# Seven block products for eight in the second output projection of a two-layer decoder step

## The chip, the cores and the metric

The kernel runs on one core of a Trainium2 chip. The metric is the device time of one execution in microseconds (us). The kernel before took 2897.57 us as the median of three runs (2897.03 to 2903.0).

## The reference, cut to what matters

One inference step of a two-layer decoder, for a prompt of 2048 positions and for 8 samples of 4 positions each, all in f32, with a model width of 1024 and a branch width of 2048. Layer 0 is gated linear attention. Layer 1 is sliding-window attention with 32 query heads in 4 groups. Each layer ends in an output projection from 2048 to 1024; the second one is the place of the change:

```python
BRANCH_WIDTH = EXPAND * D_MODEL          # 2 * 1024
...
def swa_out(o, gate, w_out):
    bsz, seq_len = o.shape[:2]
    return (o.reshape(bsz, seq_len, BRANCH_WIDTH) * jax.nn.silu(gate)) @ w_out
...
hp = hp + swa_out(swa_banded(q_p, k_p, v_p, b_sinks[j]), g_p, b_w_out[j])
...
hs = hs + swa_out(attend(q_s, k_s, v_s, pos_s, kpos_s, b_sinks[j]), g_s, b_w_out[j])
```

So for the prompt a [2048 x 2048] matrix (attention output times gate) is multiplied with `b_w_out` [2048 x 1024], the residual stream is added, and the result is the output `y`; the 32 sample rows go the same way into `ys`.

## The kernel before, in words

Every f32 operand of a large matmul is held as two f16 parts, hi and lo, and each product is three f16 matmuls (hi hi, hi lo, lo hi: `PASSES`, line 280). `split` (187) makes the parts: ScalarE (ACT) copies to hi, VectorE (DVE) or GpSimd (POOL) subtracts to lo. The prompt is cut into 16 chunks of 128 rows.

*Order of the work.* A scheduler orders the instructions of each engine by a simulated timeline; `behind` (171) lowers the priority of steps that can wait. In the attention of layer 1 the order of the matmuls is pinned to that of the program (`pin`, 1479).

1. *Layer 0* (line 895 on): 16 blocks (4 heads, 4 blocks of 512 rows each).
2. *First output projection* (1076 to 1089 and 1470): for each chunk 2 halves of 512 columns, 48 matmuls of 128x512 each. Its results are stored to `hd` and normed for layer 1.
3. *Layer 1, attention* (1501 to 1534): for 4 groups of 8 heads, 16 chunks each, so 64 blocks. While block t is attended, the query and gate projections of block t+3 are woven in as filler (`ORDER`, 1480). At the end of a block `last` (1276) makes `og`, the gated output [128 x 512] of this group; `spill_og` (617) splits it and stores hi and lo to `ogd2[c]` in DRAM (tile name oge). The last three turns of the loop have no projection left; their filler is the second output projection of chunks 0 to 2, first half.
4. *Second output projection* (1005, and 1538 to 1552): `out_steps` loads a chunk with 4 transposing DMAs (line 1012, 2 for hi and 2 for lo) and runs 16 k-tiles x 3 passes = 48 matmuls of 128x512 into one PSUM tile; `b_finish` (1481) adds the residual from `hd` and stores 512 columns of `y`. First half 0 for all 16 chunks, then half 1 for all, so 32 such units in all. The samples go through `out_sample` (1051): 4 tiles x 16 k-tiles x 2 small matmuls for each half.

*Weights ahead of time.* The weights of layer 1 are split long before they are used. `Unit.prepare` (237) gives two steps for each unit: load 256 KB of raw f32 (tile wraw, 3 buffers), split into a tile pst (2 buffers), and store that from POOL's queue (line 245) to a DRAM tile `pre`. They are taken in order from one list `prep` (835, 856): 8 steps for rope tables, 72 for the query, key, value and gate weights, 32 for `b_w_out`. `some(PR[j])` (936) takes 1, 4 or 2 of them per chunk in blocks of layer 0, 63 in all; the remaining 49 are taken 5 per chunk by chunks 4 to 13 of the first output projection (1086). `Unit.fetch` (249) loads a unit later, 512 KB at a time, into a tile W (12 buffers). Chunks 0 to 3 of the first output projection (1079 to 1083) are woven with the end of layer 0's last block and its samples, without such steps.

## Time and profile before

| | |
|---|---|
| median of 3 runs | 2897.57 us |
| the profiled execution, own time | 2899.76 us |
| its span, first to last instruction | 2898.0 us, mean granted clock of TensorE 0.989 |
| TensorE matmuls (PE) busy | 2769.2 us, 96% of the span |
| DVE, ACT, POOL busy | 1661.5, 1386.7, 1012.0 us |
| bytes moved by DMA | 393.86 MB, mean 136 GB/s |

The profile is one execution. PE is the matmul engine and PEld its weight loads, which run beside the matmuls; SP issues most DMAs. Times are counted from the first instruction. Layer 0 lasts to about 1180 us, the first output projection to about 1520 us, the attention to about 2590 us, and the second output projection alone takes the rest. A row of a view names the line of the kernel, the engine, the operation and the tiles (out<-in); "DMA share" in a table of stretches is the mean busy share of the 16 DMA engines, and can pass 1 where several transfers overlap on one.

### The profile page before, as it was taken

How to read it: one execution, taken by the hardware profiler on the slowest of the kernel's cores; microseconds unless marked ns; L12 is line 12 of the kernel's file. 1: busy time of each engine (PE TensorE's matmuls, PEld its weight loads, DVE VectorE, ACT ScalarE, POOL GpSimd, SP SyncE). 2: the span in 40 equal slices, each digit the busy share in tenths (PEclk: the TensorE clock that was granted, in tenths of full speed). 3: DMA queues.
4: the chain of work that ended last, by engine and by line, in shares of the span. 5: the costliest groups of instructions: out<-in, count | busy, mean ns of one | idle time of the engine just before them, and what ended most of it. 6: DMA issues, size and time to landing. Idle time of an engine off the chain costs nothing.

```text
span 2898.0 us, 51309 instructions
## 1 busy us (share of the span) xinstructions
PE 2769.2 (96%) x19198; PEld 1401.8 (48%) x19198; DVE 1661.5 (57%) x3543; ACT 1386.7 (48%) x3289; POOL 1012.0 (35%) x1407
## 2 busy tenths in 40 slices
PE   6899999999999999997999999999899999999999
PEld 4445444444454444444444555555555555544444
DVE  5766787687768775333214666677777767730000
ACT  6655655465556554333213555566666666620000
POOL 1241233222322221022105676566566557510000
PEclk9999999999999999998999999999999999999999
DMA  8351344124313524799866565767866777898874
GB/s 211 85 124 44 88 120 128 37 84 151 97 41 101 162 69 114 158 238 260 186 167 142 109 131 122 192 119 129 170 114 130 169 132 138 162 214 170 182 148 96
DMA packets 813331, 393.86 MB, mean 136 GB/s; under 512 B 687760, under 2 KB 740952, under 8 KB 813048
## 3 DMA queue, kind: packets, MB, share of 16 engines
q1 hardware_dynamic: 802040, 361.14, 56.3%
q0 software_dynamic: 8960, 29.37, 2.8%
q8 instruction: 150, 2.46, 0.4%
q14 instruction: 101, 0.83, 0.1%
q10 hardware_dynamic: 2080, 0.07, 0.0%
HBM read 132.61 MB, written 101.25 MB: 81 GB/s over the span
## 4 chain that ended last, share of the span: by engine, by line
PE 59%; DVE 10%; ACT 9%; DMA 9%; issue 7%; POOL 5%; SPq 1%; POOLq 0%; ACTq 0%; DVEq 0%
PE pj L99 45%; PE tr L99 6%; PE o L99 4%; PE kv L99 3%; DMA pre<-pst 2%; ACT o L1237 2%; DMA wraw<-in_a_w_in_dram 2%; DVE v L195 1%; DMA pst<-v 1%; ACT v L194 1%; PE lev L99 1%; DVE o L1232 1%; POOL pre L245 1%; DVE W L195 1%; DVE lev L1232 1%
## 5 line engine op out<-in xcount | busy, mean ns | idle before, releaser
L99 PE MATMUL pj<-W,uT 128*128 128x512 f16 x6600 | 1529.0, 381 | 6.6 <-DVE sg L475 3.4
L99 PEld LDWEIGHTS <-uT 128*128 128x128 f16 x8224 | 788.1, 98 | 892.6 <-issue 49.3
L99 PE MATMUL tr<-W,uT 128*128 128x512 f16 x1536 | 365.5, 379 | 0.0
L183 POOL TENSOR_SCALAR rs_m<-ss 128x1 f32<-128x1 f32 (+3 forms) x190 | 44.6, 235 | 757.7 <-ACT og L608 243.6
L1237 ACT ACTIVATE o<-o,mx 128x256 f32<-128x256 f32 (+1 forms) x384 | 168.6, 439 | 181.5 <-DVE mx L1232 172.1
L192 POOL TENSOR_TENSOR ogT<-og,ogT 128x512 f16<-128x512 f32 x132 | 162.1, 1228 | 168.3 <-ACT ogT L191 163.8
L99 PEld LDWEIGHTS <-X 128*128 128x128 f16 x2496 | 159.9, 98 | 120.9 <-issue 20.7
L99 PE MATMUL pj<-uT,W 128*128 128x512 f16 (+1 forms) x912 | 187.0, 356 | 27.1 <-DMA uT<-ogT 23.6
L1232 DVE CUSTOM_DVE_ANT_0 o<-o,madd,nsink 128x256 f32<-128x256 f32 (+1 forms) x384 | 184.0, 479 | 46.8 <-PE o L99 41.8
L195 DVE SCALAR_TENSOR_TENSOR v<-o,v 128x512 f16<-128x512 f32 (+1 forms) x192 | 129.0, 672 | 116.3 <-ACT v L194 98.4
L184 POOL TENSOR_TENSOR rs_r<-rs_m,mhalf 128x1 f32<-128x1 f32 (+2 forms) x186 | 185.5, 998 | 14.7
L99 PEld LDWEIGHTS <-W 128*128 128x128 f16 x2576 | 132.8, 99 | 115.0 <-issue 20.1
L1486 DVE SCALAR_TENSOR_TENSOR st<-pj,E 128x512 f32<-128x512 f32 x32 | 22.1, 692 | 269.8 <-PE pj L99 260.0
L505 POOL TENSOR_TENSOR E<-bt 128x256 f32<-128x256 f32 x96 | 74.3, 774 | 197.4 <-DVE X L192 117.7
L245 POOL DMA_DIRECT2D pre<-pst x104 | 72.3, 695 | 190.7 <-DVE pst L195 155.9
L99 PE MATMUL pj<-W,v 128*128 128x512 f16 x576 | 128.3, 379 | 0.0
L99 PE MATMUL o<-gl,X 128*128 128x256 f16 (+1 forms) x768 | 114.0, 272 | 10.2 <-DMA X<-qe 5.4
L99 PEld LDWEIGHTS <-sth 128*128 128x128 f16 x1984 | 100.3, 98 | 39.4 <-DMA sth<-v 11.2
L99 PEld LDWEIGHTS <-v 128*128 128x128 f16 x768 | 74.5, 98 | 92.6 <-issue 4.5
L646 ACT ACTIVATE ssg<-pj 128x64 f32<-128x64 f32 (+1 forms) x16 | 3.5, 240 | 236.8 <-PE pj L99 231.4
L194 ACT ACTIVATE v<-o 128x512 f16<-128x512 f32 (+1 forms) x192 | 111.3, 580 | 7.4 <-DMA sth<-v 3.7
L191 ACT ACTIVATE ogT<-og 128x512 f16<-128x512 f32 x132 | 82.2, 623 | 64.7 <-DVE og L611 44.2
(341 smaller groups left out, 4331.3 us busy)
## 6 DMA issues: line engine op xcount, KB each, us to landing
pre<-pst POOLq DMA_DIRECT2D x104, 256.0 KB, 3.8
W<-pre SPq DMA_DIRECT2D x52, 512.0 KB
ogd<-ogT SPq DMA_DIRECT2D x68, 256.0 KB
wraw<-in_a_w_in_dram SPq DMA_DIRECT2D x64, 256.0 KB
wraw<-in_b_w_in_dram SPq DMA_DIRECT2D x64, 256.0 KB
oge<-ogT SPq DMA_DIRECT2D x64, 256.0 KB
wraw<-in_a_w_out_dram SPq DMA_DIRECT2D x32, 256.0 KB
X<-in_x_prompt_dram SPq DMA_DIRECT2D x32, 256.0 KB
```

The source lines that it names most:

```text
L99: return order(nc.tensor.matmul(*a, **k))
L183: pool.tensor_scalar(m[:n, :k], ss, a, b, ALU.mult, ALU.add)
L184: pool.tensor_tensor(r[:n, :k], m[:n, :k], mhalf[:n, :k], ALU.pow)
L191: act(hi, src, AF.Copy)
L192: eng.tensor_tensor(lo, src, hi, ALU.subtract)
L194: act(hi, src, AF.Copy, scale=sc)
L195: dve.scalar_tensor_tensor(lo, src, sc, hi, ALU.mult, ALU.subtract)
L245: nc.gpsimd.dma_start(self.pre[:, :, half * 512 : half * 512 + 512], t)
L505: pool.tensor_tensor(Ev[:, :, 0, :], ref, btv[:, :, 0, :], ALU.subtract)
L1232: dve.tensor_tensor_reduce(pm[:, z], pm[:, z], madd.rearrange("p a b -> p (a b)")[:, (2 - nk) * P :], -0.125, nsink[:, g * GRP + h : g * G ...
L1237: act(pm[:, z], pm[:, z], AF.Exp, scale=-1.0, bias=nm_[:, h : h + 1], accum_out=bx["sum"][:, h : h + 1])
L1486: dve.scalar_tensor_tensor(y, pp, OSC, hr, ALU.mult, ALU.add)
```

## The change

The sixteen chunks are taken as eight pairs. With the rows of the pair's two chunks as A1 and A2, the first and second 256 of each group's 512 columns as the split of k, and the two halves of 512 output columns, the pair's product is a 2 x 2 block product, [256 x 2048] by [2048 x 1024]. It is made with seven block products for eight (a Strassen scheme in Winograd's form), each of 8 k-tiles x 3 passes = 24 matmuls of 128x512.

- *Sums of the left side* are made at the spill (`spill_forms`, for `spill_og`): an even chunk stores its two blocks as forms 0 and 1; an odd one makes the five others from its own `og` and that of the chunk before, with 4 additions of 128x256 on DVE, 3 splits (512, 512 and 256 wide) for 1, and 3 stores for 1. `og` lies in a wraw buffer now. The DRAM tile is `fd[pair]`, 7 forms.
- *Sums of the right side* are made with the weights (`form_steps`, for `prepare` of `b_w_out`): for each of 8 k-tiles one step that loads four blocks of 256 KB and seven that each make, split and store one form; four of the seven have a subtraction on POOL. So 64 steps for 32, and 56 stores of 256 KB for 32. `PR` goes from (1, 4, 2, 0) to (2, 4, 2, 0), chunks 1 to 3 of the first output projection take steps too, and each chunk takes `each` of them.
- *The products* (`Pair`): all seven right forms (2 MB each, hi and lo) stay in SBUF, three in tiles of 512 KB (W) and four in the place of uT, loaded once. Each product loads its left form with 2 transposing DMAs. The PSUM results are combined on DVE and ACT with intermediate sums in SBUF. The filler of the last three attention turns is products 0 to 5 of pair 0.
- *The samples* use forms 0 and 3 for half 0 (16 k-tiles), and forms 0, 2 and 5 for half 1 (24 k-tiles, since one block is only there as a sum).
- The scales of the attention output and of the weights are 4 and 4 times smaller (`2.0**22` for `2.0**20`, `SWB`).

```diff
-PR = (1, 4, 2, 0)
+PR = (2, 4, 2, 0)
...
-    ogd2 = [dr.tile([P, 2, BW], F16, tag=f"oge{c}", name=f"oge{c}") for c in range(NCH)]
+    fd = [dr.tile([P, 7, 2, D], F16, tag=f"fd{c}", name=f"fd{c}") for c in range(NCH // 2)]
+    wfd = [dr.tile([P, 8, 2, 512], F16, tag=f"wf{n}", name=f"wf{n}") for n in range(7)]
...
+    def spill_forms(og, old, pair, g):
+        def put(f0, src, n, eng):
+            ot = T("ogT", [P, n, 2, 256], F16, 2)
+            split((ot[:, :, 0], ot[:, :, 1]), src, eng=eng)
+            nc.sync.dma_start(fd[pair][:, f0 : f0 + n, :, g * 256 : (g + 1) * 256], ot)
+        v2 = lambda t: t.rearrange("p (f x) -> p f x", f=2)
+        if old is None:
+            put(0, v2(og), 2, pool)
+            return
+        a1, a2 = v2(old), v2(og)
+        s = v2(T("st", [P, 512], F32, 2))
+        z = v2(T("st", [P, 512], F32, 2))
+        dve.tensor_tensor(s[:, 0], a2[:, 0], a2[:, 1], ALU.add)
+        dve.tensor_tensor(s[:, 1], s[:, 0], a1[:, 0], ALU.subtract)
+        put(2, s, 2, pool)
+        dve.tensor_tensor(z[:, 0], a1[:, 0], a2[:, 0], ALU.subtract)
+        dve.tensor_tensor(z[:, 1], a1[:, 1], s[:, 1], ALU.subtract)
+        put(4, z, 2, dve)
+        put(6, a2[:, 1:], 1, dve)
...
-    wob = [out_w(i["b_w_out"][0], half, None) for half in range(2)]
-    prep = [f for w in gw + wob for f in w.prepare()]
+    UP = [4 * (m // 2) + m % 2 for m in range(8)]
+    def form_steps(m):
+        b, f = {}, {}
+        def load():
+            for n, (r, z) in enumerate(((0, 0), (0, 1), (1, 0), (1, 1))):
+                t = T(("wraw", "wraw", "qT", "kT")[n], [P, 512], F32, 3 if n < 2 else 1)
+                k = UP[m] + 2 * r
+                nc.sync.dma_start(t, i["b_w_out"][0][k * P : (k + 1) * P, z * 512 : z * 512 + 512])
+                b[r, z] = t
+            f[0], f[3], f[5] = b[0, 0], b[1, 0], b[1, 1]
+        def put(n):
+            def sub(x, y):
+                t = T("sth", [P, 512], F32, 2)
+                pool.tensor_tensor(t, x, y, ALU.subtract)
+                f[n] = t
+            if n == 2:
+                sub(b[0, 1], b[0, 0])
+            elif n == 1:
+                sub(b[1, 1], f[2])
+            elif n == 4:
+                sub(b[1, 1], b[0, 1])
+            elif n == 6:
+                sub(b[1, 0], f[1])
+            t = T("pst", [P, 2, 512], F16, 2)
+            split((t[:, 0], t[:, 1]), f[n], SWB)
+            nc.gpsimd.dma_start(wfd[n][:, m], t)
+        return behind([load] + [lambda n=n: put(n) for n in (0, 2, 1, 3, 6, 5, 4)], 200)
+    prep = [f for w in gw for f in w.prepare()] + [f for m in range(8) for f in form_steps(m)]
...
+    each = (len(prep) + tail) // tail
     aout[0][0]()
     todo = []
     for c in range(lead):
-        todo += [aout[c + 1][0]] + aout[c][1][0] + aout[c][1][1]
+        todo += [aout[c + 1][0]] + mix(aout[c][1][0] + aout[c][1][1], some(each if c else 0))
...
-        weave(aout[c][1][0] + aout[c][1][1], some(5))
+        weave(aout[c][1][0] + aout[c][1][1], some(each))
...
-                og = T("og", [P, 512], F32, 1)
-                dve.scalar_tensor_tensor(og, bx["po"].rearrange("p h d -> p (h d)"), 1.0 / (PB * 2.0**20), self.sg, ALU.mult, ALU.mult)
-                spill_og(og, ogd2[self.c], g, pool)
+                og = self.og = T("wraw", [P, 512], F32, 3)
+                dve.scalar_tensor_tensor(og, bx["po"].rearrange("p h d -> p (h d)"), 1.0 / (PB * 2.0**22), self.sg, ALU.mult, ALU.mult)
+                spill_forms(og, self.prev.og if self.c % 2 else None, self.c // 2, g)
...
+    PRODS = ((0, "pj"), (3, "tr"), (2, "o"), (1, "pj"), (4, "tr"), (5, "o"), (6, "tr"))
+    wf = {}
+    def wform_big(n):
+        t = T("uT", [P, 8, 2, 512], F16, 4)
+        nc.sync.dma_start(t, wfd[n])
+        wf[n] = lambda k, hl, s=ALL: t[:, k, hl, s]
+    def wform(n):
+        ts = []
+        for x in range(4):
+            t = T("W", [P, 2, 2, 512], F16, NW)
+            nc.sync.dma_start(t, wfd[n][:, 2 * x : 2 * x + 2])
+            ts.append(t)
+        wf[n] = lambda k, hl, s=ALL: ts[k // 2][:, k % 2, hl, s]
...
+    def left(pair, n):
+        f = PRODS[n][0]
+        if pair == 0 and n < 4:
+            t = T("W", [P, 2, 8, P], F16, NW)
+            ts = [t[:, 0], t[:, 1]]
+        elif pair == 0 and n < 6:
+            ts = [T(tag, [P, 8, P], F16, 2 if tag == "bt" else 1) for tag in (("qT", "kT"), ("bt", "bt"))[n - 4]]
+        else:
+            tags = (("v", "sg"), ("sth", "pst"), ("v", "sg"), ("X", "ogT"), ("v", "sg"), ("qe", "ke"), ("v", "sg"), ("sth", "pst"), ("X", "ogT"), ("qe", "ke"))[turn[0] % 10]
+            turn[0] += 1
+            ts = [T(tag, [P, 8, P], F16, 4 if tag in ("v", "sg") else 2) for tag in tags]
+        for hl in range(2):
+            nc.sync.dma_start(ts[hl], fd[pair][:, f, hl], transpose=True)
+        return ts
+    class Pair:
+        def __init__(self, p):
+            self.p, self.l, self.b = p, {}, {}
+        def load(self, n):
+            self.l[n] = left(self.p, n)
+        def add(self, tag, bufs, pp, t):
+            d = T(tag, [P, 512], F32, bufs)
+            dve.scalar_tensor_tensor(d, pp, OSCB, t, ALU.mult, ALU.add)
+            return d
+        def y(self, c, half, pp, t):
+            cs = slice(half * 512, half * 512 + 512)
+            hr = T("E", [P, 512], F32, 2)
+            nc.sync.dma_start(hr, hd[c][:, cs])
+            dve.tensor_tensor(hr, hr, t, ALU.add)
+            nc.sync.dma_start(o["y"][0, c * P : (c + 1) * P, cs], self.add("st", 2, pp, hr))
+        def steps(self, n):
+            tag = PRODS[n][1]
+            c0, c1 = 2 * self.p, 2 * self.p + 1
+            todo = [(k, a, b) for k in range(8) for a, b in PASSES]
+            box = []
+            def step(part):
+                if not box:
+                    box.append(PT(tag, [P, 512], bufs=2))
+                for x in part:
+                    k, a, b = todo[x]
+                    mm(box[0], self.l[n][a][:, k, :], wf[n](k, b), start=x == 0, stop=x == 23)
+            def fin():
+                pp = box[0]
+                if n == 0:
+                    self.s1 = T("og", [P, 512], F32, 1)
+                    act(self.s1, pp, AF.Copy, scale=OSCB)
+                elif n == 1:
+                    self.u2 = self.add("Sh", NG, pp, self.s1)
+                elif n == 2:
+                    self.p5 = pp
+                    self.v = self.add("S", 1, pp, self.u2)
+                elif n == 3:
+                    self.y(c0, 0, pp, self.s1)
+                elif n == 4:
+                    self.u3 = self.add("Sh", NG, pp, self.u2)
+                    self.y(c1, 1, self.p5, self.u3)
+                elif n == 5:
+                    self.y(c0, 1, pp, self.v)
+                else:
+                    self.y(c1, 0, pp, self.u3)
+            return [lambda x=x: step(range(x, x + 4)) for x in range(0, 24, 4)] + [fin]
...
+            x = 2 * (n - TOT)
+            fill = pairs[0].steps(x) + pairs[0].steps(x + 1)
...
-            run(gw[g + 1].steps() if g + 1 < NKV else wob[0].steps())
-        if n in (NKV * NCH - 5, NKV * NCH - 2, NKV * NCH):
-            bout[(n - NKV * NCH + 6) // 3][0]()
+            if g + 1 < NKV:
+                run(gw[g + 1].steps())
+        if n in (TOT - 8, TOT - 5, TOT - 3):
+            wform_big((0, 1, 2)[(TOT - 8, TOT - 5, TOT - 3).index(n)])
+        if n == TOT - 2:
+            for x in range(3):
+                pairs[0].load(x)
+        if n == TOT:
+            wform_big(3)
+            pairs[0].load(3)
+            wform(4)
+            pairs[0].load(4)
+        if n == TOT + 1:
+            wform(5)
+            pairs[0].load(5)
+        if n == TOT + 2:
+            wform(6)
+            pairs[0].load(6)
...
-    run(out_steps(wob[0], 0, ogd2, b_finish, 3))
...
-    wo, wo1 = wob
-    for c in range(4, NCH):
-        run(out_steps(wo, 0, ogd2, b_finish, c))
-        if c == 10:
-            run(wo1.steps())
-    run(out_sample(wo, 0, b_finish_s))
-    for c in range(NCH):
-        run(out_steps(wo1, 1, ogd2, b_finish, c))
-        if c == 8:
-            run(out_sample(wo1, 1, b_finish_s))
+    prods = [(p_, n) for p_ in range(NCH // 2) for n in range(7)][6:]
+    AHEAD = 6
+    for p_, n in prods[1 : AHEAD]:
+        pairs[p_].load(n)
+    left8, right8 = UP, [k + 2 for k in UP]
+    for x, (p_, n) in enumerate(prods):
+        if x + AHEAD < len(prods):
+            p2, n2 = prods[x + AHEAD]
+            pairs[p2].load(n2)
+        run(pairs[p_].steps(n))
+        if n == 6 and p_ in (3, 5):
+            cols = [slice(z * P, (z + 1) * P) for z in range(4)]
+            if p_ == 3:
+                fs, kts = (0, 3), left8 + right8
+            else:
+                fs, kts = (0, 2, 5), left8 + left8 + right8
+            run(out_sample([lambda k, hl, z=z, fs=fs: wf[fs[k // 8]](k % 8, hl, z) for z in cols], p_ // 5, b_finish_s, kts, OSCB))
```

40 lines of the change are left out of this document (14 added, 26 removed).

## The prediction

> **What bounds the kernel now.** I read the page's engine line first, then stretches of 20 us in the stages that the change touches, then the waits of the matmul engine there, then single rows.
>
> ```profile
> PE 2769.2 (96%) x19198; PEld 1401.8 (48%) x19198; DVE 1661.5 (57%) x3543; ACT 1386.7 (48%) x3289; POOL 1012.0 (35%) x1407
> ```
>
> PE sets the time on average, so taken-out matmuls count in full wherever PE is never kept waiting. The stretches (PE, PEld, DVE, ACT, POOL busy, clock, DMA share, GB/s) show where that is so:
>
> ```profile
> 1300.00:1320.00 20.00, 17.29 (x74) 7.58 (x74) 6.86 (x11) 6.84 (x13) 5.40 (x8) 0.91 0.96 280
> 1320.00:1340.00 20.00, 16.70 (x116) 8.07 (x115) 6.92 (x11) 5.29 (x10) 4.91 (x8) 1.00 0.97 250
> 1340.00:1360.00 20.00, 6.85 (x196) 6.62 (x192) 6.41 (x11) 7.02 (x14) 5.41 (x8) 0.66 0.88 225
> ...
> 2420.00:2528.00 108.00, 105.08 (x876) 58.96 (x874) 79.00 (x205) 70.60 (x204) 70.98 (x87) 0.98 0.80 144
> 2540.00:2560.00 20.00, 16.47 (x136) 8.56 (x134) 11.51 (x35) 10.44 (x31) 3.80 (x7) 1.00 1.15 209
> 2560.00:2580.00 20.00, 17.05 (x146) 9.37 (x145) 7.12 (x19) 6.44 (x21) 3.57 (x7) 1.00 1.05 208
> ...
> 2680.00:2700.00 20.00, 20.00 (x95) 9.06 (x93) 0.75 (x2) 0.00 (x0) 0.00 (x0) 1.00 0.78 158
> ```
>
> There are four regimes. In the second output projection alone (last row) PE is full at clock 1.00, DVE nearly idle and DMA at 0.78: bound by PE alone. In the passage into it (2540 to 2580) DMA is over 1 and PE loses 20 - 16.47 + 20 - 17.05 = 6.5 us. In the late attention PE is at 97% with DVE at 79.00/108 = 73%. In the first output projection PE loses 2.7 + 3.3 + 13.1 = 19.2 us from 1300 to 1360, and most of that is one wait on VectorE:
>
> ```profile
> PE pj L99 <- DVE st L1031: 18.1, 3, 12.9
> ```
>
> The matmuls leave the first regime; the work that is added falls into the other three. So the gain is sharp and its costs are vague.
>
> **The change part by part.**
>
> *Matmuls taken out.* Two evictions that are eleven units of 48 matmuls apart:
>
> ```profile
> 2606.70 0.69 DVE L1486 SCALAR_TENSOR_TENSOR st<-pj,E 128x512 f32<-128x512 f32 x1 [9.67 <-PE pj L99]
> ...
> 2720.66 0.69 DVE L1486 SCALAR_TENSOR_TENSOR st<-pj,E 128x512 f32<-128x512 f32 x1 [9.67 <-PE pj L99]
> ```
>
> (2720.66 - 2606.70)/11 = 10.36 us a unit, 215.8 ns a matmul. Before there are 32 x 48 = 1536, after 8 x 7 x 24 = 1344. 192 go: 192 x 0.2158 = 41.4 us less. The chain at the very end stays: last matmul, one eviction of 0.69 us, one store of 256 KB; the addition of the residual and the intermediate sum is done earlier.
>
> *Samples.* Half 1 takes 24 k-tiles for 16: 4 tiles x 8 x 2 = 64 small matmuls more.
>
> ```profile
> 2720.46 3.65 PE L99 MATMUL pj<-ogTs,W 128*128 128x64 f16 x128
> 2723.95 4.91 PE L99 MATMUL pj<-W,uT 128*128 128x512 f16 x22
> ```
>
> 128 of them take 2723.95 - 2720.46 = 3.49 us, so 64 add 1.7 us.
>
> *The projection alone, other resources.* Each 24 matmuls (5.18 us) need 2 transposing DMAs, as 48 needed 4: the same rate. In 10.36 us at a share of 0.78 the DMA engines work 8.1 us for 4 transposes, one load and one store of 256 KB. For plain transfers I take a stretch in which only weights are fetched:
>
> ```profile
> 1505.00:1513.00 8.00, 8.00 (x39) 3.64 (x38) 0.69 (x1) 0.00 (x0) 0.00 (x0) 1.00 1.00 397
> ```
>
> At 397 GB/s, 262 KB take 0.66 us; so a transpose takes (8.1 - 1.3)/4 = 1.7 us. A pair then needs 14 x 1.7 + 8 x 0.66 = 29.1 us of DMA in 7 x 5.18 = 36.3 us, a share of 0.80. PE hides it; the combining on DVE too (four residual additions, seven evictions, some 0.7 us each, so 8 us of 36). I cost this at nothing. Without that cover the price is that of the fourth rival.
>
> *Sums at the spill (attention, 32 odd blocks).* The rows for the added work:
>
> ```profile
> L508 DVE TENSOR_TENSOR E<-E,kT x96: 409/421/2474, 65.4 to 1081.4; 128x256 f32<-128x256 f32 x96
> ```
>
> ```profile
> L192 DVE TENSOR_TENSOR qe<-kT,qe x64: 639/998/1770, 1548.2 to 2540.7; 128x512 f16<-128x512 f32 x64
> ```
>
> ```profile
> L191 ACT ACTIVATE ogT<-og x64: 617/619/632, 1592.8 to 2584.0; 128x512 f16<-128x512 f32 x64
> L192 POOL TENSOR_TENSOR ogT<-og,ogT x64: 1142/1158/1191, 1594.4 to 2584.7; 128x512 f16<-128x512 f32 x64
> L620 SPq DMA_DIRECT2D oge<-ogT x64: 558/559/1408, 1598.4 to 2587.3; - x64
> ```
>
> DVE gains 4 additions of 256 columns and the lo parts of 512 and of 256 columns. In attention, where POOL works beside it, the 512-wide subtraction takes 1.0 us in the median against 0.64 at least; I price the 256-wide ones at half of that, 0.5. So 5 x 0.5 + 1.0 = 3.5 us; at the minima it would be 5 x 0.41 + 0.64 = 2.7 us. ACT gains a hi of 512 and one of 256 columns, about 1.0 us; POOL keeps its one subtraction; SP issues two stores more, 1.1 us. The Trainium skill (GPSIMD Engine Reference, § 1 Specifications) says that GpSimd's SBUF interfaces are shared with VectorE and contended by VectorE instructions with two SBUF inputs. This speaks against the change, as all the added work on DVE is of that form; the spread from 0.64 to 1.77 us agrees, and by the rule none of it would run at the minima. With the minima the 5 us taken below would be 5 x 2.7/3.5 = 3.9, and the sum 2871.
>
> Is it hidden? A block in the late attention lasts:
>
> ```profile
> 2500.57 0.56 SPq L620 DMA_DIRECT2D oge<-ogT  x1
> ...
> 2513.93 0.58 SPq L620 DMA_DIRECT2D oge<-ogT  x1
> ```
>
> 13.4 us between spills. DVE at 73% is free for 3.6 us of it, just the 3.5 added in every second block, and the even block is free as before. What is queued behind: DVE's score maxima (L1232) for the next block, ACT's exponentials behind these, then the transposes of the probabilities, for which the values matmuls wait in PE's pinned order; and ACT, in the third split, waits for one of only two ogT buffers to be stored. From the scores to the values that need them there is about one block of other matmuls, so a delay of 1 to 3 us is mostly swallowed. But it is not always so now:
>
> ```profile
> PE kv L99 <- DMA sth<-v: 5.8, 4, 2.0
> PE kv L99 <- DMA pst<-v: 4.5, 5, 1.5
> ```
>
> Nine waits of 1.1 us between 2000 and 2500. Bounds: nothing, or all 3.5 us in each of 32 blocks, 112 us. Below nothing is excluded apart from og's third buffer, since work is only added. I take 5 us, by the nearest row: five more such waits of 1 us. The stores grow from 16.8 MB to 29.4 MB; 12.6 MB at 397 GB/s are 32 us over 1070, 0.03 more of DMA share.
>
> *Passage.* The weights before the first product ran were half of `b_w_out`, 4.2 MB; now 14.7 MB of forms come between block 56 and product 6. Forms 0 to 2 (5.3 us each at 397 GB/s) lie in blocks with a DMA share of 0.80. Forms 3 to 6 can't start before the last projection has read its tiles: 8.4 MB, 21 us; beside them 8 transposes of left forms (14 us) and 8 of the last probabilities (14 us), 49 us. PE has until product 6: 6 x 5.18 = 31 us of products, and the attention of the last blocks, about (13.4 - 10.36) x 3 = 9 us: 40 us. 9 us short, less what can be drawn ahead, against 6.5 us that PE loses here now. Bounds: the loss goes (-6.5) or the whole of it plus the three early left forms (6 x 1.7 = 10 us) is exposed, 19 us for 6.5, so +12.5. I take +5.
>
> *Weight forms.* Before, 49 steps remain for the first output projection; after, 144 - 72 = 72, of which 64 split and store. Their pace and their work on ACT and DVE now:
>
> ```profile
> L194 ACT ACTIVATE pst<-wraw x32: 612/629/631, 1300.7 to 1401.2; 128x512 f16<-128x512 f32 x32
> L195 DVE SCALAR_TENSOR_TENSOR pst<-wraw,pst x32: 670/692/708, 1301.4 to 1401.9; 128x512 f16<-128x512 f32 x32
> ```
>
> ```profile
> L245 POOL DMA_DIRECT2D pre<-pst x49: 686/687/732, 1243.4 to 1402.9; - x49
> ...
> DMA to landing us min/median/max: 2.7/4.5/7.0
> ```
>
> (1402.9 - 1243.4)/48 = 3.3 us a step: a chain over two pst buffers, where ACT waits until a store has landed. A chunk of 20.7 us (2 x 10.36) holds 5 x 3.3 = 16.6 us of it now, after 5.25 x 3.3 = 17.4 us. It stays under 20.7, but the steps sit in DVE's queue ahead of the evictions that PE waits for; the 12.9 us wait is that. Transfers per chunk fall: 6 steps move 0.75 x 4 loads + 5.25 stores = 8.25 x 256 KB, against 10. With about the same density over 12 chunks for 10, the loss grows by 19.2 x 2/10 = 4 us; four POOL subtractions of 1.2 us per 8 steps are hidden, as POOL is busy 27% (5.41 of 20 us). Bounds: the loss of 19.2 us vanishes, as transfers fall, or doubles. I take +4. The nine further steps in layer 0 (`PR`) I cost at nothing: 0.63 us of ACT and 0.69 us of DVE each, on engines that are busy 48% and 57%, spread over three heads; shown in full they would be 12 us.
>
> **Sum.** -41.4 + 1.7 + 5 + 5 + 4 = -25.7 us. The profiled execution's own time is 2899.76, 2.2 us over the median of 2897.57; it becomes 2874.1, and the median 2871.9, so 2872.
>
> **Rivals.**
>
> *Stalls in the first projection go* (faster still). Fewer transfers per chunk and steps from chunk 1 on take the 12.9 us wait away: +4 becomes -13, which gives 2855. For it: DMA at 0.96 there. Against: the steps are in a chain over two buffers that stays.
>
> *The forms come late in the passage.* +15 instead of +5: the full deficit, and probabilities' transposes queued behind 2 MB loads. 2882. For it: DMA over 1 there already. Against: SP's order lets forms 0 to 2 come eight blocks earlier.
>
> *DVE bounds the odd blocks* (slower). Place: the sums stand in DVE's queue ahead of the next block's score maxima, and push everything behind them. If half of the 3.5 us shows in each of 32 blocks: 56 for 5, so -41.4 + 1.7 + 56 + 5 + 4 = +25.3 us, 2923. It decides from (41.4 - 1.7 - 9)/32 = 0.96 us exposed per odd block. For it: 3.5 added where 3.6 are free. Against: blocks of group 0 are longer, even blocks have room, and PE has a block's work between cause and effect.
>
> *The tail becomes bound by DMA* (the change does not do what it says). If a transpose takes 2.5 us with nothing but transposes queued, a pair needs 14 x 2.5 + 5.3 = 40.3 us, not 36.3: 7 x 4.0 = 28 us back, 2900. For it: SP issued single transposes in up to 10.9 us:
>
> ```profile
> L1012 SPq DMA_TRANSPOSE uT<-oge x128: 1232/1316/10867, 2361.8 to 2859.4; - x128
> ```
>
> Against: that is in the passage; at 0.78 nothing waited.
>
> **How the numbers follow.** My sum 0.53, first projection without stalls 0.14, late forms 0.12, DVE 0.14, DMA tail 0.07. 0.2%, about what a measurement of this kernel can tell from no change, is 5.8 us. Faster: 0.53 + 0.14 + 0.12 = 0.79; same: 0.07; slower: 0.14. The range leaves out the slower rival. Low: all 19.2 us of the first projection's loss gone, 2872 - 23 = 2849. High: the tail rival, 2900, or late forms with 0.7 us per odd block (22 for 5), 2899; with the runs' own spread, 2848 to 2902.
>
> **What would show it.** PE has 192 fewer 128x512 matmuls, and products end every 5.18 us from start to end with PE full. The waits of PE on the probabilities' transposes grow by about 5 us, not by 30; DVE in 2420 to 2528 goes from 73% to about 86%. Around product 6 of pair 0 PE waits for a form or a left form by some 10 us. In the first projection waits on L1031's counterpart total about 23 us. I am wrong if products lie more than 5.3 us apart (a DMA tail), if the late attention's block exceeds 14.4 us in odd turns, or if steps of the forms run past 4 us each and PE loses over 40 us before the attention.

## The result and the profile after

The kernel after takes 2994.55 us (median of 4 runs, 2988.36 to 2996.53), the kernel before 2899.61 us in the same comparison (4 runs, 2897.03 to 2903.0). The ratio is 1.032, with a 95% interval of 1.030 to 1.034: slower by 3.2%, where 2872 us was forecast, 0.9% faster. The profiled execution has a span of 2992.9 us against 2898.0, so 94.9 us have to be found.

The engine line of the page of after:

```profile
PE 2776.3 (93%) x19070; PEld 1399.7 (47%) x19070; DVE 1847.0 (62%) x3815; ACT 1440.2 (48%) x3385; POOL 1080.2 (36%) x1463
```

PE has 19198 - 19070 = 128 matmuls fewer, as 192 large ones less 64 small ones should give. Yet it is busy for 7 us more, at a share of 93% for 96%: the work left PE, and PE waits more and is granted a lower clock (0.971 in the mean for 0.989).

**Where the time went.** The stages are marked by rows that both kernels have: the stores of the first projection's result (`hd`), and the values matmuls of the attention (kv<-rmask,sth). First before, then after (minimum, median and maximum in ns, then the first and the last start in us):

```profile
L1032 SPq DMA_DIRECT2D hd<-E x16: 319/327/1410, 1167.2 to 1508.2; - x16
L1032 SPq DMA_DIRECT2D hd<-st x16: 319/529/1697, 1174.6 to 1533.5; - x16
L99 PE MATMUL kv<-rmask,sth x1984: 192/193/203, 1581.1 to 2582.9; 128*128 128x64 f16 x199
```

```profile
L1080 SPq DMA_DIRECT2D hd<-E x16: 320/327/617, 1181.3 to 1544.3; - x16
L1080 SPq DMA_DIRECT2D hd<-st x16: 319/529/570, 1190.7 to 1568.6; - x16
L101 PE MATMUL kv<-rmask,sth x1984: 192/193/242, 1617.2 to 2709.2; 128*128 128x64 f16 x199
```

The first `hd` store ends layer 0 here, the last one ends the first projection, and the last values matmul ends the attention with its passage into the second projection. The same marks for the builds of the experiments (us, one profiled execution each):

| build | layer 0 | first projection | to attention | attention, passage | rest | span |
|---|---|---|---|---|---|---|
| before | 1167.2 | 366.3 | 47.6 | 1001.8 | 315.1 | 2898.0 |
| after | 1181.3 | 387.3 | 48.6 | 1092.0 | 283.7 | 2992.9 |
| after less before | +14.1 | +21.0 | +1.0 | +90.2 | -31.4 | +94.9 |
| e1_third_buffer | 1183.7 | 385.1 | 48.7 | 1087.5 | 280.5 | 2985.5 |
| e2_no_sums | 1181.4 | 388.8 | 48.5 | 1064.4 | 283.8 | 2966.9 |
| e3_one_spill | 1187.1 | 385.8 | 49.2 | 1021.5 | 276.3 | 2919.9 |
| e4_before_forms_spilled | 1168.6 | 368.3 | 48.8 | 1068.6 | 316.1 | 2970.4 |
| e5_lo_on_pool | 1184.4 | 385.8 | 48.7 | 1054.4 | 280.2 | 2953.5 |
| e6_all_on_pool | 1179.1 | 384.4 | 48.7 | 1048.8 | 277.4 | 2938.4 |
| e11_none_on_pool | 1180.8 | 388.0 | 49.2 | 1087.0 | 280.1 | 2985.1 |
| e7_pr_back | 1171.6 | 390.2 | 47.9 | 1088.1 | 283.1 | 2980.9 |
| e8_no_late_forms | 1188.7 | 384.1 | 48.5 | 1068.5 | 283.3 | 2973.1 |
| e9_four_buffers | 1181.3 | 375.8 | 48.8 | 1100.7 | 281.0 | 2987.6 |
| e10_no_weight_sums | 1181.9 | 376.2 | 49.4 | 1095.4 | 283.7 | 2986.6 |
| c1_combined | 1170.7 | 377.3 | 48.8 | 1060.8 | 275.9 | 2933.5 |
| c2_passage | 1172.2 | 373.7 | 49.0 | 1041.8 | 289.9 | 2926.6 |
| g1_sums_in_tail | 1167.9 | 377.6 | 48.8 | 1013.9 | 307.9 | 2916.1 |

The rest got shorter, as forecast. The attention with the passage got longer by nearly three times that. Stretches of after (PE, PEld, DVE, ACT, POOL busy, clock, DMA share, GB/s); the first is 800 us of the attention, and the 800 us of before from its first values matmul on follow in the second fence:

```profile
1617.00:2417.00 800.00, 741.37 (x6301) 413.41 (x6300) 596.65 (x1459) 474.85 (x1383) 498.17 (x634) 0.97 0.66 139
...
2660.00:2680.00 20.00, 16.07 (x122) 8.48 (x122) 11.11 (x30) 6.40 (x18) 1.32 (x2) 0.91 1.10 216
2680.00:2700.00 20.00, 9.47 (x55) 4.49 (x52) 4.27 (x10) 4.62 (x15) 2.60 (x4) 0.74 1.00 206
...
2760.00:2780.00 20.00, 20.00 (x95) 9.05 (x93) 3.79 (x6) 0.60 (x1) 0.00 (x0) 1.00 0.79 156
```

```profile
1581.00:2381.00 800.00, 773.04 (x6823) 435.67 (x6822) 547.00 (x1412) 480.35 (x1435) 514.29 (x675) 0.99 0.68 138
```

In the attention PE stands idle for 58.6 us of 800 where it was 27.0, with a clock of 0.97 for 0.99. Estimated over 1000 us from these two rows that is 40 us of waits and 20 us of clock. VectorE goes from 68% to 75% busy: no engine is full, and DMA is no busier (0.66 for 0.68). This speaks for a chain that became longer, and not for a resource that ran out. Why the clock is lower no run shows. In the passage (2660 to 2700) PE loses 14.5 us of 40 with DMA at 1.0 to 1.1; in the second projection it is full again.

**Where in the attention.** The loss is not spread evenly. Take the start of the first values matmul of each of the 64 blocks in both traces. Of the first 59 intervals between them, 34 are as long in after as in before to within 0.2 us, among them 12 of the 18 that took 13.5 us. Another 15 are 1.7 to 7.6 us longer, 69.9 us together, where the 59 as a whole are 65.5 us longer; the other 24.7 of the 90.2 us come behind them, in the passage. Of the 29 intervals that follow the sums of an odd block, 17 are among the 34. So more than half of the odd blocks swallow the added work, and the others don't.

**The chain in an odd block.** The added instructions on VectorE in after, from 1600 to 2640 us:

```profile
L640 DVE TENSOR_TENSOR st<-wraw x30: 415/880/971, 1653.1 to 2624.2; 128x256 f32<-128x256 f32 x30
L643 DVE TENSOR_TENSOR st<-wraw,wraw x30: 416/420/958, 1653.5 to 2625.1; 128x256 f32<-128x256 f32 x30
L641 DVE TENSOR_TENSOR st<-st,wraw x30: 417/1479/1491, 1654.3 to 2625.4; 128x256 f32<-128x256 f32 x30
L644 DVE TENSOR_TENSOR st<-wraw,st x30: 418/1007/1481, 1654.8 to 2628.4; 128x256 f32<-128x256 f32 x30
L195 DVE TENSOR_TENSOR ogT<-st,ogT x30: 673/780/1644, 1658.2 to 2630.1; 128x512 f16<-128x512 f32 x30
L195 DVE TENSOR_TENSOR ogT<-wraw,ogT x30: 415/425/426, 1661.8 to 2635.1; 128x256 f16<-128x256 f32 x30
```

One and the same addition takes 0.42 us at least and 1.48 us in the median at L641. The medians add up to 5.0 us; the prediction had 3.5. One odd block, in order of time (start, duration):

```profile
2113.37 1.44 POOL L1190 TENSOR_TENSOR kT<-kT,S 128x512 f32<-128x512 f32 x1
...
2113.61 1.48 DVE L641 TENSOR_TENSOR st<-st,wraw 128x256 f32<-128x256 f32 x1
...
2115.12 0.63 ACT L194 ACTIVATE ogT<-st 128x512 f16<-128x512 f32 x1 [1.05 <-DVE st L641]
...
2117.86 1.38 POOL L1319 TENSOR_TENSOR sg<-sg,rv 128x512 f32<-128x512 f32 x1 [0.88 <-DVE rv L1317]
...
2118.26 1.53 DVE L195 TENSOR_TENSOR ogT<-st,ogT 128x512 f16<-128x512 f32 x1
```

Work out the ends. POOL's L1190 ends at 2114.81 and L641 at 2115.09; L1319 at 2119.24 and the 512-wide subtraction at 2119.79. Each time VectorE's instruction began later than POOL's and ended 0.28 (256 wide) or 0.55 us (512 wide) after it: it stood until POOL's was done, and then ran. This holds over the attention: 29 of the 30 instructions of L641 in the window began during one of POOL's, and all 29 ended 0.28 to 0.29 us after it. Where POOL does nothing, in the second projection of the last build below (g1), none of the same additions is long:

```profile
L1595 DVE TENSOR_TENSOR bt<-wraw,bt x28: 415/424/427, 2632.9 to 2823.2; 128x256 f32<-128x256 f32 x28
```

The Trainium skill (SBUF — State Buffer, § SBUF: two separate sides) says of a GpSimd instruction that reads SBUF and a VectorE instruction with two SBUF inputs that the one that starts first holds a shared pair of ports for its whole instruction, and that the other is fully blocked. The trace agrees, with these pairs. ACT stood for 1.05 us behind one of them, and in the sum over the attention of after (waits of ACT: total, times, longest):

```profile
ACT ogT L194 <- DMA fd<-ogT: 47.1, 28, 5.7
ACT ogT L194 <- DVE st L641: 31.9, 29, 2.6
...
ACT ogT L194 <- DVE st L644: 24.3, 25, 1.8
```

Before, ScalarE's copy to ogT waited for 2.2 us in all, on `og`. Behind these copies in ACT's order stand the exponentials of the next scores. PE's waits in the same stretch of after are not on the transposes that the prediction watched (3.3 and 0.8 us):

```profile
PE o L101 <- DVE mxs L1475: 12.6, 5, 3.6
PE o L101 <- DVE v L198: 11.9, 14, 2.1
PE tr L104 <- ACT skv L1372: 9.5, 3, 4.7
...
PE tr L104 <- DVE sK L1424: 8.4, 3, 3.8
PE kv L101 <- DVE wraw L1328: 6.8, 3, 2.9
...
PE kv L101 <- DMA sth<-v: 3.3, 1, 3.3
...
PE kv L101 <- DMA pst<-v: 0.8, 2, 0.5
```

In before, from 1560 to 2530 us, there is none on v, and:

```profile
PE tr L102 <- DVE sK L1375: 4.8, 3, 1.7
PE o L99 <- DVE mxs L1426: 4.8, 5, 2.0
PE tr L102 <- ACT skv L1323: 4.7, 3, 1.6
```

L198 makes the lo part of the probabilities and so is the last reader of the score tile in PSUM: there PE is held up where it wants to write the next scores, by VectorE that is late. But mxs, skv and sK are tiles of the samples' attention, whose steps are woven into some of the blocks, and the waits on wraw, on ogT and on sK in other rows come at matmuls of the samples or behind such a tile. Together these are 49.1 of the 74.2 us that the view lists, for 15.8 of 29.8 in before. The kernel before with nothing but the spill of after added (e4 below) shows the same, 55.0 of 71.0. So what the spill delays is above all the chain of the samples. That is read from these rows; no run here leaves the samples out.

### The profile page after: what moved, and what is told of

It is laid out like the page before. It is cut to its first block, busy times and chain, and to the rows that moved or that the text cites. A ratio compares the mean times of both kernels' runs of the same rounds, so it can differ in the third digit from the quotient of the medians.

```text
span 2992.9 us, 51869 instructions
## 1 busy us (share of the span) xinstructions
PE 2776.3 (93%) x19070; PEld 1399.7 (47%) x19070; DVE 1847.0 (62%) x3815; ACT 1440.2 (48%) x3385; POOL 1080.2 (36%) x1463
## 5 line engine op out<-in xcount | busy, mean ns | idle before, releaser
L101 PE MATMUL pj<-W,uT 128*128 128x512 f16 x5064 | 1210.0, 385 | 6.5 <-ACT qT L430 2.1
L101 PEld LDWEIGHTS <-uT 128*128 128x128 f16 x6944 | 649.9, 99 | 731.1 <-issue 71.8
L101 PEld LDWEIGHTS <-X 128*128 128x128 f16 x2656 | 176.2, 98 | 171.7 <-issue 46.8
L198 DVE SCALAR_TENSOR_TENSOR v<-o,v 128x512 f16<-128x512 f32 (+1 forms) x192 | 128.8, 671 | 109.3 <-ACT v L197 97.2
L101 PEld LDWEIGHTS <-v 128*128 128x128 f16 x1088 | 106.8, 99 | 142.5 <-issue 18.9
L101 PEld LDWEIGHTS <-sth 128*128 128x128 f16 x2144 | 117.7, 99 | 67.1 <-DMA sth<-v 19.2
L195 POOL TENSOR_TENSOR ogT<-og,ogT 128x512 f16<-128x512 f32 x68 | 88.3, 1298 | 156.4 <-ACT ogT L194 151.9
L101 PEld LDWEIGHTS <-sg 128*128 128x128 f16 x832 | 81.3, 99 | 106.4 <-issue 12.7
L101 PE MATMUL kv<-rmask,sth 128*128 128x64 f16 x1984 | 106.9, 194 | 17.1 <-DMA sth<-v 17.1
L101 PE MATMUL pj<-W,sg 128*128 128x512 f16 x504 | 114.2, 384 | 2.9 <-DVE E L1079 2.9
L101 PE MATMUL kv<-rmask,pst 128*128 128x64 f16 x992 | 102.0, 194 | 5.2 <-DMA pst<-v 5.0
```

The lines of the kernel that those rows point to most:

```text
L101: return order(nc.tensor.matmul(*a, **k))
L195: eng.tensor_tensor(lo, src, hi, ALU.subtract)
L198: dve.scalar_tensor_tensor(lo, src, sc, hi, ALU.mult, ALU.subtract)
```

## The experiments

Each time below is one execution's (the four of after lie between 2988.36 and 2996.53), and the kernel before took 2897.56 to 2900.89 us on the same chips. My theory after the result (A) was that ScalarE's wait for one of two ogT buffers is the cost, because it is the largest single new wait; the rival (B) was that VectorE's added work with its dependent chain is. The stages of two builds with the same code for a stage differ by up to some 10 us, since the scheduler arranges every build anew (layer 0 of after and of e8: 1181.3 and 1188.7), so a few us in one stage prove nothing.

### The spill undone, and done alone

In e3 only the 512-wide split of the second chunk is left in an odd block; the sums, the two other splits and their stores are left out, and the products read four left forms for seven:

```diff
-        dve.tensor_tensor(s[:, 0], a2[:, 0], a2[:, 1], ALU.add)
...
-        put(2, s, 2, pool)
+        put(2, a2, 2, pool)
...
-        put(4, z, 2, dve)
-        put(6, a2[:, 1:], 1, dve)
...
-        f = PRODS[n][0]
+        f = PRODS[n][0] % 4
```

> An odd block stores its two blocks as an even one does (one split, one store, no sums), and the products read four left forms in place of seven: leaves out the left sums. The weight forms, the seven products and their combining stay. If the spill is the whole of the attention's loss, by either theory, the attention is as long as before (110 us less), and the time is 2994 - 110 = 2884. A rival, that the bigger transfers and the loads of forms lengthen the attention: less than 60 us come back, 2935 or more.

Measured 2921.69 us, 73 less than after: neither the 110 that the theory gave nor the rival's under 60. Up to the passage the attention of e3 is as long as that of before (1.6 us shorter over the 59 intervals). e4 is the kernel before with the spill of after and nothing else of it:

```diff
-                spill_og(og, ogd2[self.c], g, pool)
+                spill_forms(og, self.prev.og if self.c % 2 else None, self.c // 2, g)
...
-                nc.sync.dma_start(ot[q], ogs[c][:, q % 2, q // 2 * D : q // 2 * D + D], transpose=True)
+                nc.sync.dma_start(ot[q], fd[c // 2][:, c % 2 * 2 + q // 2, q % 2], transpose=True)
```

> The kernel before with the spill of the change alone: odd blocks make the sums and store three times, and the projection of before reads two of the forms for each chunk; the output is not the product. Weights, matmuls and the order of everything else are those of before. If the spill alone costs the 110 us: 2898 + 110 = 3008. If the loss in the attention comes from the spill and something else of the change together: 2930 to 2980.

Measured 2972.25 us against 2897.56. By the spans the spill costs 2992.9 - 2919.9 = 73.0 us taken away and 2970.4 - 2898.0 = 72.4 us added: about the same from both sides, 2.3 us per odd block in the mean (by the column of the attention alone 70.5 and 66.8 us). That is the failed term, and it hardly depends on the rest of the change. The 110 us that both expectations took for the attention's loss are 90.2 in the table, with the passage; so the time is in the second range, and what the spill leaves of the 90.2 is in the passage. The values matmuls of e4 and e3, to be held against those of before (to 2582.9) and after (to 2709.2):

```profile
L99 PE MATMUL kv<-rmask,sth x1984: 192/193/204, 1585.7 to 2654.3; 128*128 128x64 f16 x199
```

```profile
L101 PE MATMUL kv<-rmask,sth x1984: 192/193/242, 1622.1 to 2643.6; 128*128 128x64 f16 x199
```

### Which part of the spill

e1 gives the third split a buffer of its own:

```diff
-            ot = T("ogT", [P, n, 2, 256], F16, 2)
+            ot = T("og", [P, n, 2, 256], F16, 1) if f0 == 6 else T("ogT", [P, n, 2, 256], F16, 2)
```

> The third store of an odd block gets a buffer of its own (og's place, which lies idle in the attention); nothing else changes. Theory A, ScalarE's queue: in the attention ScalarE stands 47.1 us, 28 times, until an ogT buffer has been stored, and behind it stand the exponentials of the next block. Then this wait falls to under 10 us and the attention (first to last spill of the attention stage, 110 us longer than before) gets some 35 to 50 us shorter; the whole about 2950. Theory B, VectorE's load: the 3.5 us of additions and subtractions on VectorE per odd block are what counts, wherever ScalarE waits; then the time stays within 10 us of 2994.

Measured 2987.33 us, some 7 less. ACT's wait for an ogT buffer is 7.8 us now, and VectorE's wait for ScalarE's hi part, 35.4 us in after, is 0.2. Theory A falls: waits of 47 and 35 us in total were worth 7 us at most, and even these 7 are not clear of after's own spread, whose lowest run is 2988.36. e2 leaves out the four additions and splits what is there already:

```diff
-        dve.tensor_tensor(s[:, 0], a2[:, 0], a2[:, 1], ALU.add)
...
-        put(2, s, 2, pool)
+        put(2, a2, 2, pool)
...
-        put(4, z, 2, dve)
+        put(4, a1, 2, dve)
```

> Leaves out the four additions on VectorE that make the sums at the spill, so five of the seven left forms are plain blocks; splits, stores, buffers and everything else stay. Theory B (VectorE's load): the 4 x 0.5 = 2 us in each of 32 odd blocks come back, and ScalarE's waits on the sums (56 us) with them: 60 us or more, about 2930. Theory A (the wait for an ogT buffer): that wait stays at about 47 us, and of the rest only a part shows: 2965 to 2980.

Measured 2968.73 us, 26 less, where theory B had 60 or more. By this run the additions are a good third of the cost, the three splits and stores the rest. Then the place of the work was changed, with e1's buffer kept. e5 makes the lo parts on POOL:

```diff
-        put(4, z, 2, dve)
-        put(6, a2[:, 1:], 1, dve)
+        put(4, z, 2, pool)
+        put(6, a2[:, 1:], 1, pool)
```

> The third buffer, and only the two lo parts on GpSimd; the four sums stay on VectorE. All on GpSimd gave 47 us beyond the buffer. In the change the four additions took 0.88, 1.48, 0.42 and 1.00 us in the median (0.42 alone), the lo parts 0.78 and 0.43. If the additions on VectorE are dear because they meet GpSimd's instructions, more work on GpSimd makes them no cheaper, and most of the gain needs the sums to move: 2965 to 2985 here. If the lo parts, for which VectorE waited 35 us on ScalarE's hi parts, are the larger share: 2945 to 2960.

Measured 2955.57 us, 32 less than e1 and in the second range. But VectorE's wait for ScalarE's hi parts can't be the reason, as it was gone in e1. e6 has the additions on POOL too (`pool.tensor_tensor` in all four):

> The third buffer of the run before it, and all the arithmetic that the spill adds (four sums, two lo parts) on GpSimd in place of VectorE; what is computed stays the same. Theory: what lengthens the attention is VectorE's queue, in which each odd block puts 3.5 us of work and waits for ScalarE ahead of the next block's score maxima. Then most of the spill's 73 us come back beyond the 7 us of the buffer alone: 2935 or less, and the attention's values matmuls span under 1050 us (1092 in the change). Rival: ScalarE's two more hi parts and the chain of three splits count, on whichever engine the rest runs: 2965 to 2990. Second rival: GpSimd, now with about 6 us more per odd block, holds the rotary part of the queries back and nothing is gained: 2985 or more.

Measured 2940.24 us, another 15 less; the attention is under 1050 us as expected, the time 5 us over. On POOL an addition takes 0.73 us, and it hardly varies:

```profile
L641 POOL TENSOR_TENSOR st<-st,wraw x31: 714/725/751, 1653.3 to 2613.8; 128x256 f32<-128x256 f32 x31
```

So 47 of the 73 us go when the added work leaves VectorE (2987 to 2940), although the four additions aren't shorter on POOL: their medians add up to 2.91 us there and to 2.39 us in e1. Nor does the gain go by the time that left VectorE: 2.2 us per odd block by the medians for the 32 us of e5, 2.7 us for the 15 us of e6. That it is the place ahead of the next score maxima that counts is argued, not shown. The attention of e6 is still 27 us longer than that of e3 (1048.8 to 1021.5). Ahead of the passage PE waits there for ogT at the samples' values matmuls, 17.8 us in all, where e3 lists no such wait: the samples' probabilities lie in the same two ogT buffers as the parts of the spill. e11 goes the other way and puts the last POOL subtraction of the odd block on VectorE:

```diff
-        put(2, s, 2, pool)
+        put(2, s, 2, dve)
```

> The third buffer for the 256-wide part kept, and the one subtraction of the odd blocks' spill that was left on GpSimd (128x512) put on VectorE as well, so that the odd blocks' whole spill, four additions and three lo parts, is on VectorE. If the additions are long because of the spill's own GpSimd subtraction beside them, their medians (0.88, 1.48, 0.42 and 1.01 us) fall to 0.42 to 0.5 each, 2 us less in 32 blocks, which outweighs 0.64 us more: attention shorter by some 20 us, 2955 to 2970. If they are long because of GpSimd's other work (the splits of the projections), the medians stay, VectorE gets 0.7 to 1 us more in every odd block, and the time rises by 15 to 30 us over the build with the third buffer, 3000 to 3015. Together with the build that has everything on GpSimd (2940) this gives the price of the place from both ends.

Measured 2987.09 us, against 2987.33 for e1: no difference, and neither of the two outcomes. The rows tell why the first fails: the two longest stay as they were in e1 (0.89 and 1.48 us there), so what VectorE waits for there isn't the spill's own subtraction but other work on POOL. Only L644, which had that subtraction beside it, falls, from 0.66 to 0.41:

```profile
L640 DVE TENSOR_TENSOR st<-wraw x30: 412/904/969, 1653.9 to 2619.2; 128x256 f32<-128x256 f32 x30
...
L644 DVE TENSOR_TENSOR st<-wraw,st x30: 406/412/989, 1657.6 to 2623.8; 128x256 f32<-128x256 f32 x30
...
L195 DVE TENSOR_TENSOR og<-wraw,og x30: 416/1482/1492, 1655.2 to 2620.4; 128x256 f16<-128x256 f32 x30
```

And one subtraction more on VectorE (0.68 us in 30 blocks) cost nothing that shows. As L644 got shorter and POOL had 1.16 us less per odd block, this alone doesn't prove that VectorE's busy time costs nothing.

### The passage and the weights

e8 leaves out the loading of right forms 4 to 6, 6.3 MB of the passage; the products with them read form 3 (`wf[n] = wf[3]` in `wform`):

> Leaves out the loading of the right forms 4, 5 and 6 (6.3 MB): the products with them read form 3 instead. All matmuls, spills and stores stay. Theory for the passage: these loads, with those of form 3 and the left forms, hold back the transposes of the last blocks' probabilities, and 20 to 25 us of the 25 that the matmul engine stands between 2640 and 2740 come back: 2970. Rival: what stands in the passage is the pile of left forms' transposes and the order in which SP takes them: less than 8 us come back, 2987 or more.

Measured 2975.09 us, 5 over what the theory gave; the attention with its passage is 23.5 us shorter. Of these, 7.1 us come in the 59 intervals ahead of the first load that is left out, where both builds have the same code; 16.4 lie in the passage. The waits of PE from 2620 us on in after, and SP's issues there:

```profile
PE kv L101 <- DMA sth<-v: 13.9, 4, 7.8
PE kv L101 <- DMA pst<-v: 4.2, 4, 1.5
```

```profile
2643.62 1.48 SPq L1543 DMA_DIRECT2D W<-wf  x3
...
2645.67 0.60 SPq L1536 DMA_DIRECT2D uT<-wf  x1
...
2647.05 8.78 SPq L1292 DMA_TRANSPOSE sth<-v  x1
```

```profile
L1292 SPq DMA_TRANSPOSE sth<-v x10: 1232/1244/8781, 2605.7 to 2701.4; - x10
```

The transpose of the probabilities, for which the values matmuls wait, is issued 1.4 us behind a load of 2 MB (form 3) and occupies SP for 8.78 us, where the median of the ten from 2605 us on (last row) is 1.24 us. Three loads of 512 KB of the late forms were issued just ahead of that one, and a fourth behind it. e8 keeps form 3 and leaves those out: its longest transposes of the probabilities from 2580 us on take 4.05 (sth) and 5.85 us (pst), for 8.78 and 4.49 in after, and PE's waits on the probabilities' transposes from 2600 us on fall from 18.1 to 9.1 us. So the late forms are a cause, and 9 of the 16 us are seen in these waits.

e7 takes the nine steps out of layer 0 again:

```diff
-PR = (2, 4, 2, 0)
+PR = (1, 4, 2, 0)
...
-    each = (len(prep) + tail) // tail
+    each = 5
```

> Takes the nine steps out of layer 0 again (one a chunk in the first blocks, as before) and takes 5 steps per chunk in the first output projection for 6, with the rest at its end. If the 14 us that layer 0 lost are those nine steps: layer 0 ends within 4 us of 1167, the first projection loses about as much as in the change (387 us) or up to 10 more, as it has more to do, and the whole is 2975 to 2990. If layer 0 lost them to something else: it still ends at about 1181, and the time is 2990 or more.

Measured 2982.67 us: 12 less, layer 0 9.7 shorter. That this is no accident of the schedule the table shows: in the four builds with (1, 4, 2, 0) layer 0 takes 1167.9 to 1172.2 us, in the ten with (2, 4, 2, 0) 1179.1 to 1188.7. The cover that was named for these steps, engines busy 48% and 57%, did not hide them. e9 gives the steps four tiles for two, e10 leaves out their subtractions on POOL, so that four of the seven forms are copies of a block:

```diff
-            t = T("pst", [P, 2, 512], F16, 2)
+            t = T("qe" if n in (2, 3, 5) else "pst", [P, 2, 512], F16, 2)
```

```diff
-                pool.tensor_tensor(t, x, y, ALU.subtract)
-                f[n] = t
+                f[n] = x
```

> The split weight forms alternate between pst and the two idle buffers of qe, so four of them can be on their way to be stored instead of two. In the change ScalarE stands 74.9 us, 33 times, for a stored pst buffer in the first output projection. Theory: the steps' chain over two buffers, standing in VectorE's queue ahead of the evictions, makes the 21 us that the first projection lost. Then these waits fall under 25 us, the first projection takes about 366 us as before or less, and the whole about 2970. Rival: the transfers themselves or the loads of four blocks at once limit it: the stage stays over 380 us and the time over 2985.

> Leaves out the 32 subtractions on GpSimd that make the right forms: four of seven forms are copies of a block. Splits, stores and their number stay. If the subtractions in the steps' chain make the loss of the first output projection: it takes 366 to 374 us (387 in the change) and the whole 2975 to 2982. If the chain waits on the stores alone, as the four buffers' run with its 11 us says: within 6 us of 387, and the whole 2988 or more.

Measured 2989.42 and 2988.36 us. In each the first projection is 11 us shorter (375.8 and 376.2), and most of it is lost again in an attention of the same code that is 8.7 and 3.4 us longer: inconclusive for the total, and short of the 366 us that e9's theory gave for the stage. The cause in the stage stays open. ACT's wait for a tile to be stored is 81.8 us in after (first line) and 40.8 + 16.6 with four tiles, but in e10, where the stage is as short, it is 95.2 us, and in before it was 76.1 (each from 1180 to 1600 us):

```profile
ACT pst L197 <- DMA wf<-pst: 81.8, 36, 5.7
```

```profile
ACT pst L197 <- DMA wf<-pst: 40.8, 17, 6.5
...
ACT qe L197 <- DMA wf<-qe: 16.6, 7, 3.6
```

### Towards a faster version

c1 joins e6, e7 and e9. c2 adds another order to c1: the filler of the last turns is products 0 and 1 of the first two pairs, then 2 and 3 of the first, so that forms 4 and 5 are fetched one turn later.

> The changes that helped, together: third buffer, spill arithmetic on GpSimd, the nine steps out of layer 0 with 5 a chunk, four buffers for the weight forms. If they add up: 2994.5 - 54 - 12 - 11 = 2917, still slower than before by 0.7%, with the passage's loss left. If the schedules interfere: 2925 to 2935.

> As the combined one, with another order in the passage: the last three attention turns take products 0 and 1 of pairs 0 and 1 and then 2 and 3 of pair 0, so the right forms 4, 5 and 6 are needed only after the attention, and the product whose PSUM tile is kept no longer takes one of the two o banks from the last scores. Theory of the passage (late forms ahead of the probabilities' transposes, 20 us; the o bank, some 5 more): 15 to 25 us under the combined one, 2895 to 2902, about as fast as before. Rival (the number of bytes in these 60 us sets the time, in any order): less than 8 us under it.

Measured 2935.36 and 2928.72 us (before: 2900.71). In c1 the gains don't add up: it is 18 us over their sum. c2 is 6.6 us under c1, as its rival said. Its attention is 19 us shorter than c1's and its rest 14 longer: the loss mostly moved on. g1 spills `og` as f32 and makes the sums of pairs 1 to 7 in the second projection, where VectorE is nearly idle:

```diff
+        if pair > 0:
+            nc.sync.dma_start(ogf[2 * pair + odd][:, g], og)
...
-        run(pairs[p_].steps(n))
+        weave(pairs[p_].steps(n), side[x])
```

> The same arithmetic in another place: for pairs 1 to 7 the attention only spills og in f32 beside the three forms that are plain blocks, and the four sums and their splits are made on VectorE and ScalarE beside the products, where both stand nearly idle; pair 0 keeps its sums at the spill (on GpSimd). The last three attention turns take products 0 and 3 of pairs 0 to 2, which need no sums and only two of the right forms. The weight side is that of the combined run. Theory: the sums cost what the stage in which they stand lets them cost; in the projection alone nothing waits for these engines. Then the attention (first to last values matmul) is within 20 us of before's 1002, the rest about 277, and the whole 2880 to 2892, faster than before. Rival: the added 2 MB of loads per pair push the DMA share of the tail over 1, or products wait for their left forms: products lie more than 5.4 us apart and the time is 2900 or more.

Measured 2918.01 us (before: 2898.89), over the 2892 of the theory. The attention is back to within some 12 us of before, as it should be if the stage sets the price of the same sums. But the rest is 307.9 us, for 276 to 284 in the builds with after's order of products. A stretch of g1, and PE's two longest waits from 2608 us on:

```profile
2620.00:2880.00 260.00, 238.96 (x1355) 110.79 (x1356) 126.97 (x298) 47.33 (x118) 0.00 (x0) 0.95 0.91 201
```

```profile
PE tr L104 <- DVE ssg L679: 7.5, 1, 7.5
PE tr L101 <- DMA v<-X: 7.2, 1, 7.2
```

All waits on left forms together are 17.2 us, with DMA at 0.91 (the rival had it over 1), and 7.5 us are the samples' projection waiting for VectorE. This speaks against the sums being free here. This is the best version found, and it is still 0.7% slower than before. Whether these some 30 us can be hidden stays open.

## Why the prediction was wrong

*Matmuls taken out: right.* -41.4 + 1.7 = -39.7 was forecast for products and samples; e3, without the spill's cost, has a rest 38.8 us shorter than before. Two evictions of after one pair apart:

```profile
2772.40 0.69 DVE L1574 SCALAR_TENSOR_TENSOR Sh<-tr,og 128x512 f32<-128x512 f32 x1 [3.81 <-PE tr L101]
...
2808.66 0.69 DVE L1574 SCALAR_TENSOR_TENSOR Sh<-tr,og 128x512 f32<-128x512 f32 x1 [3.81 <-PE tr L101]
```

36.26 us for seven products, 5.18 each, PE full and DMA at 0.79 (0.80 forecast). The tail bound by DMA is refuted.

*Sums at the spill: the failed step, a term mis-sized.* "I take 5 us, by the nearest row: five more such waits of 1 us." It measured 73, 2.3 us per odd block in the mean. Its bounds, nothing and 112 us, held it; the choice between them did not. Three things in it were wrong:
- The price of a 256-wide addition was taken as half of a 512-wide one, 0.5 us. The median at L641 was 1.48, because what is added is the rest of POOL's instruction, whatever the width of one's own. The Trainium skill's rule in the prediction (GPSIMD Engine Reference, § 1 Specifications) spoke against the change and is borne out, though L643 ran at its minimum in the median (0.42 us); it was given 1 us, between 3.9 and 5.
- The 5 us took all blocks as alike. That "a delay of 1 to 3 us is mostly swallowed" had no row behind it; for more than half of the odd blocks it came true, as 17 of the 29 intervals behind them did not grow. But 15 intervals grew by 1.7 to 7.6 us, where five waits of 1 us had been put down: by PE's waits above all where the delay meets the samples' steps, which the prediction's term leaves out.
- The waits that were to show it, on the probabilities' transposes, fell instead (5.8 + 4.5 us from 1560 to 2530 in before, 3.3 + 0.8 in after). PE waited at the scores and, for the greater part, at the samples' steps.

The rival "DVE bounds the odd blocks" had the place and the sign, with 56 us; its point of decision, 0.96 us in each odd block, was passed more than twice over. It had been given 0.14. The range left it out, and the time came beyond its upper end, 2902.

*Passage: the mechanism of a rival, the size too small.* +5 was taken, +15 in the rival on late forms. In after the passage is 24.7 us longer than in before; with the spill cut down (e3) attention and passage are still 19.7 us longer, and e8 gives back 16.4 us there. The queueing of the probabilities' transposes behind loads of forms is in the rows.

*Weight forms: too small.* +4 was forecast and +21.0 measured in the first projection. The waits on the counterpart of L1031 are 24.2 us (about 23 forecast), 4.5 more than in before; what was left out were the others that came with it, 14.4 us for 1.0. PE from 1180 to 1600 us in after:

```profile
PE pj L101 <- DVE st L1079: 12.2, 3, 8.5
PE pj L101 <- DVE E L1079: 12.0, 3, 5.0
PE lev L101 <- ACT ssm L194: 5.8, 1, 5.8
```

*Layer 0: costed at nothing, +14.1 measured*, of which e7 gives back 9.7. "Shown in full they would be 12 us" was the better value.

Against before, e3, which has all but the spill's cost, gives +19.9 in layer 0, +19.5 in the first projection, +1.6 to the attention, +19.7 for the passage and -38.8 behind it, +21.9 together; with 73.0 for the spill that is the 94.9. The cause inside the 73 is settled only in part. Shown are the whole of it (e3 and e4), that 47 us of it go when its arithmetic leaves VectorE (e1 to e6), and that VectorE's additions stand behind POOL's other instructions. Not settled is how the 47 us divide between that blocking and the mere place in VectorE's order; that the collision with the samples' chain is what makes the delay show is read from the waits and not tested; and of the 27 us that stay when everything is on POOL, PE's 17.8 us of waits for the samples' ogT are a part that the rows show.

## What to carry to other kernels

Work that is saved in a stage bound by one engine counted in full here, but work that is moved into a stage with a chain over four engines was paid for by the delay of the chain and not by the free share of an engine. So don't price it by one typical block: more than half of the odd blocks here swallowed the added work, and the loss came for the greater part where a second chain is woven in. Compare block by block, and look for such blocks first. Ask also in which stage the same sums cost less; g1 had most of the attention back by moving them, and then met the next limit. And a long total of one wait is no price: the largest new wait here, 47 us, was worth 7 at most.

## What the runs showed of the hardware

An addition of 128x256 in f32 with two SBUF inputs takes 0.42 us on VectorE by itself and up to 1.49 us when it begins during an instruction of GpSimd; when it is held up, it ends 0.28 us after that instruction. The same addition takes 0.73 us on GpSimd, between 0.71 and 0.75 but for single cases: beside a busy GpSimd a single one can be the quicker there (1.48 us on VectorE at L641 in after), though four together were not (2.91 us in e6, 2.39 in e1). A transpose by DMA that SP issues in 1.24 us in the median took 8.78 us among loads of 2 MB and four times 512 KB.
